# Table blocks as dot products on VectorE, and two of an expert's 42 weight tiles multiplied whole in fp32

## The chip, the cores and the metric

The kernel runs on one core of a Trainium2 chip. The metric is the device time of one execution in microseconds (us): the median of three runs is 1449.65 (1448.9 to 1453.23). The engines are named as in the profile: PE is TensorE's matmuls and PEld its weight loads, DVE is VectorE, ACT is ScalarE, POOL is GpSimd, SP the engine that issues most transfers. A difference of about 0.3% (4.3 us) is what a measurement of this kernel can tell from no change.

## The reference, cut to what matters

Everything is float32. Two layers work on 256 latent tokens of width 1024. In each layer six vectors of 1024 come out of a conditioning vector `c` (the "ada table"); they shift, scale and gate what follows. Layer 0 is differential attention with a short convolution, then a dense SwiGLU (the FFN). Layer 1 is a spatial gating unit (the SGU), then eight SwiGLU experts, of which each token uses two.

```python
def ada_chunks(cond, w, b):                  # w: 1024 x 6144 per layer
    m = jax.nn.silu(cond) @ w + b
    return jnp.split(m, 6, axis=-1)

def moe_swiglu(h, router_w, wg, wu, wd):     # wg, wu: 8 x 1024 x 3584, wd: 8 x 3584 x 1024
    ...
    for e in range(N_EXPERTS):
        out = out + dense_gate[..., e:e + 1] * swiglu(h, wg[e], wu[e], wd[e])
    return out
```

## The kernel before

**Split products.** A weight tile is 128 x 2048 fp32 (1 MB in `raw`, brought by SP's queue). ACT rounds it to fp32r (the high part, `mh`), DVE subtracts to get the low part (`ml`), and PE multiplies in fp32r: high by high, high by low, low by high (`mm3`, L141 to L144), three products of 512 columns for each 128 x 512 piece.

**The experts** (L912 to L1338). Each has 42 tiles: in each of 7 chunks of 512 hidden columns two tiles of the gate matrix, two of the up matrix, and two of the down matrix, which is multiplied two chunks later (LAG = 2). One chunk's six tiles make a step: gate, up, down. An expert with at most 64 tokens is *light*: its tokens' high and low parts stand side by side as 128 columns, so two products do the work of three (`products`, L1083, lines L1089 and L1090). Otherwise it is *heavy* (lines L142 to L144). PE chooses between the two by a branch at each group of two tiles. Here the experts run in the order heavy, light, light, light, heavy, heavy, light, light. After a chunk's gate and up products the 128 x 512 results are turned (L1156 light, L1158 heavy), made into `m_sg` (L1162 on ACT, L1163 on DVE) and split into `moe_aT` (L217, L218). Tokens for the next expert are gathered in chunks 4 and 5 (`m_oh` L1110, `m_pg` L1119, `m_xg`); results are put back early in the next expert (`m_yg`, `m_sc`, `moe_acc`).

**Buffers.** Raw tiles stand in a ring of six (five of `raw`, slot 8). High parts have five buffers (four of `hi`, and slot 7 where n % 5 is 4), low parts five. So the high part of tile n goes into the buffer of tile n - 5. `Weights.split` (L948) is called up to three tiles ahead of the group, `Weights.load` six tiles ahead of the split. Each engine takes its instructions in the order in which they stand; SP issues a load when DVE has freed its raw buffer.

**The table.** Of the 24 blocks of 512 columns, eight are multiplied on DVE during the FFN (GROUPS, the entries with a last 0; `ada_v`, L332): rows of the table lie on the partitions, so a half block of 4 x 512 columns takes four operations that multiply by one value of silu(c) per partition and add to a running sum (L341, L343), and when both halves are done four small matmuls with a column of ones add up over the partitions (L349), and DVE adds the bias (L351).

Of the kernel before, what the change touches and what calls it, by code (L numbers as in the profile page):

```python
# [37 lines left out]
BEFORE_FFN, BEFORE_SGU = 1, 3  # L38

STAGES = ((0, 2), (2, 4), (4, 6), (6, 8))  # L40

# [33 lines left out]
def hybrid_kernel(  # L75
    ctx: ExitStack, tc: tile.TileContext, consts, params, heads, x_t, ctx_t, sgu_ws_t, router_t, ada_b, sgu_b_s,
    ada_w, ada_pairs, w_qk, w_in_even, w_out_even,
    ffn_w_gate, ffn_w_up, ffn_w_down, sgu_w_in, sgu_w_out,
# [170 lines left out]
    waiting, due = [], [0.0]  # L249
    gf1 = gp.tile([P, D], F32, name="gf1")  # L250

# [54 lines left out]
    def ada(blocks, n):  # L306


        layer, n0 = blocks[0]
        nb, b = len(blocks), n - n0  # L310
        if b == 0:
            held[0] = bank(f"ada{layer}_{n}", psd)
        pa = held[0]
        ada_mm(pa, cS[:, :, 3 - b:35 - b], None, layer, n, b == 0, b == nb - 1)
        if b < nb - 1:
            flush()
            return
# [4 lines left out]
        nc.sync.dma_start(gf1, ada_b[1:2, 5 * D:6 * D].partition_broadcast(P))  # L322

        def gate():
            for o in range(2):
                T.matmul(pa, selb[o], rw, start=True, stop=True)
                v = gf1[:, o * 512:o * 512 + 512]
                V.tensor_tensor(v, pa, v, op=ALU.add)

        waiting.append(gate)  # L330

    def ada_v(layer, n, half):  # L332

        r = ada_load(layer, n, half)
        if half == 0:
            held[0] = next_rows()
        ac = held[0]
        for j in range(4):
            k = 4 * half + j
            if k == 0:  # L340
                V.tensor_scalar(ac, r[:, j, :], cT[:, k, 0:1], None, op0=ALU.mult)  # L341
            else:
                V.scalar_tensor_tensor(ac, r[:, j, :], cT[:, k, 0:1], ac, op0=ALU.mult, op1=ALU.add)  # L343
        flush()
        if half:
            def cols_of():
                pa = bank(f"adv{layer}_{n}_c", psd)
                for i in range(4):
                    T.matmul(pa[:, i:i + 1], ac[:, i * P:(i + 1) * P], ones[:, 0:1], start=True, stop=True)  # L349
                c = R_ADA + layer * 48 + n * 4  # L350
                V.tensor_tensor(modT[:, layer, n // 2, (n % 2) * 4:(n % 2) * 4 + 4, 0], pa[:, :4], cols[:, c:c + 4], op=ALU.add)  # L351

            waiting.append(cols_of)

# [274 lines left out]
    for s, (k0, k1) in enumerate(STAGES):  # L629
# [4 lines left out]
        if s == 0:  # L634
            nc.sync.dma_start(trig, consts[:, C_COS:C_W])
            nc.sync.dma_start(early[:, 256:640], heads.partition_broadcast(P))
        modulated(ctxT, rc, m_c, hc, k0, k1, "xc")
        w = split(qk, f"qk{k0}")
# [277 lines left out]
    class Weights:  # L916

        def __init__(self):  # L920
            self.tiles, self.groups, self.raw, self.parts = [], [], {}, {}
            for e in range(NE):
                for ci in range(NCH):
                    for m in range(2):
                        self.add([((moe_w_gate, moe_w_up)[m][e, ci, half], 4) for half in range(2)])
                    if e or ci >= LAG:
                        self.add(self.down(*divmod(e * NCH + ci - LAG, NCH)))
# [4 lines left out]
            self.loads = self.splits = 0  # L932

# [7 lines left out]

        def load(self, upto):
            while self.loads < min(upto, len(self.tiles)):
                n = self.loads
                self.raw[n] = load(*self.tiles[n], f"mw{n}", None if n % 6 < 5 else 8)
                self.loads += 1

        def split(self, upto):  # L948
            while self.splits < min(upto, len(self.tiles)):
                n = self.splits  # L950
                self.load(n + 1)
                r = self.raw.pop(n)
# [5 lines left out]
                self.parts[n] = hi, lo  # L958
                self.splits += 1

# [136 lines left out]
    class Expert:  # L1097


        def __init__(self, e, pos, xg_slot, n):  # L1100
            self.e, self.n, self.pos = e, n, pos
            self.aT, self.part = {}, {}
            self.xg = in_pairs(slot(xg_slot, n + "_xg", F32R)[:, :2 * KT * P], KT)
# [56 lines left out]
        def act(self, ci, pts):  # L1160
            sg = x2k(f"{self.n}_{ci}_sg")
            A.activation(sg, pts[0], AF.Silu)  # L1162
            V.tensor_tensor(sg, pts[1], sg, op=ALU.mult)  # L1163

            def cut():
                self.aT[ci] = in_pairs(at[((self.e * NCH if isinstance(self.e, int) else 0) + ci) % 3], 4)
                split_pairs(self.aT[ci], sg)

            return cut

        def down(self, ci, parts, light):
            aT = self.aT[ci]
# [12 lines left out]
        def gated(self, i):  # L1185
            src = x2k(f"{self.n}_yg{i}")
            V.tensor_tensor(src, self.y[i], gf1[:, i * 512:(i + 1) * 512], op=ALU.mult)
            return src
# [32 lines left out]
    behind["V"] = ex.made.ins  # L1221
    W.load(8)
    lights = [None] * NE
# [6 lines left out]
    def group(light, body):  # L1230
# [3 lines left out]
        for n in range(tiles.stop + 1, tiles.stop + 4):  # L1234
            W.split(n)
            W.load(n + 6)
            if n == tiles.stop + 2:
# [144 lines left out]
def laid_out(inputs):  # L1382
# [8 lines left out]
    pairs = i["ada_w"][0, :, :2 * D].reshape(2, 4, P, 2, 4, 256).transpose(4, 0, 2, 1, 3, 5).reshape(4, 2, P, 2048)  # L1391

    def ffn_up(w):
        whole = tiles(w[0, :, :2560], 4, 512).transpose(1, 0, 2, 3).reshape(10, P, 2048)
# [4 lines left out]
             "sgu_ws_t": i["sgu_w_s"][0].transpose(2, 0, 1), "router_t": i["router_w"][0].reshape(KT, P, NE).transpose(1, 0, 2),  # L1399
             "ada_b": i["ada_b"], "sgu_b_s": i["sgu_b_s"],  # L1400
             "ada_w": tiles(i["ada_w"], 4, 512), "ada_pairs": pairs,
             "w_qk": tiles(w_in[:, :1024], 2, 1024), "w_in_even": tiles(w_in[:, 1024:], 4, 512), "w_out_even": tiles(i["w_out_even"][0], 4, 512),
# [21 lines left out]
```

## Time and profile before

The page is of one execution that took 1453.82 us, with a span of 1452.0 us between its first and last instruction.

| engine | busy us | share of the span |
|---|---|---|
| PE | 1382.3 | 95% |
| PEld | 1149.5 | 79% |
| DVE | 1213.6 | 84% |
| ACT | 986.2 | 68% |
| POOL | 1.9 | 0% |

The shares are means over stages with different limits: the first 209 us are attention and convolution, the FFN runs to about 400 us, the SGU to about 508 us, and the experts fill the rest. TensorE's granted clock is 0.99 of its upper level (2.4 GHz) over the span. Busy time of pipelined matmuls counts each from its start to its modelled end, so the distance between the starts of two matmuls in a row is what one costs PE.

### The profile page before, as it was taken

The page shows a single profiled execution, that of the slowest core. Times are in us where ns is not written, and L with a number is a line of the kernel's source. Part 1 is how long each engine was busy: PE and PEld are TensorE (multiplying, and loading weights), DVE is VectorE, ACT ScalarE, POOL GpSimd, SP SyncE. Part 2 cuts the span into 40 slices and gives each one's busy share as a digit, 9 for nine tenths or more (in the row PEclk, how much of TensorE's full clock was granted, in tenths as well). Part 3 has the DMA queues.
Part 4 walks back from the last instruction along what each step waited for, and adds up shares of the span by engine and source line. Part 5 has one row for each costly group of instructions (what it writes and reads, how often), then busy time and mean ns, then how long its engine had stood idle before and what let it go on. Part 6 is the DMA issues. An engine that isn't in the chain of part 4 may idle for free.

```text
span 1452.0 us, 19805 instructions
## 1 busy us (share of the span) xinstructions
PE 1382.3 (95%) x7746; PEld 1149.5 (79%) x7746; DVE 1213.6 (84%) x1208; ACT 986.2 (68%) x927; POOL 1.9 (0%) x7
## 2 busy tenths in 40 slices
PE   6999999999999999998998998999999999999896
PEld 4667789999979788886777876778888888777674
DVE  5687588776667597789999999999888888999997
ACT  3444354334355587787898988987787678798895
POOL 0000000000000000000000000000000000000000
PEclk9999999999999999999999999999999999999999
DMA  9654388877664588899999999999999889999994
GB/s 374 230 212 179 139 343 320 304 266 267 232 230 176 218 342 343 321 375 353 401 403 398 402 407 406 385 412 354 362 327 351 327 332 359 400 397 401 407 404 184
DMA packets 66783, 473.52 MB, mean 326 GB/s; under 512 B 7376, under 2 KB 7760, under 8 KB 9696
## 3 DMA queue, kind: packets, MB, share of 16 engines
q1 hardware_dynamic: 66464, 471.16, 83.3%
q8 instruction: 93, 1.52, 0.4%
q0 software_dynamic: 192, 0.56, 0.2%
q14 instruction: 34, 0.28, 0.1%
HBM read 470.64 MB, written 1.05 MB: 325 GB/s over the span
## 4 chain that ended last, share of the span: by engine, by line
PE 62%; DVE 18%; issue 8%; ACT 8%; DMA 4%; SPq 0%; DVEq 0%; ACTq 0%
DVE ml L957 12%; PE m L144 5%; PE m L142 5%; PE m L143 5%; ACT mh L956 5%; PE fg_ps L164 4%; PE fd L164 4%; PE fu_ps L164 4%; PE m_y L142 3%; PE m_y L144 3%; PE m_y L143 3%; PE ada L259 2%; PE so_ps L164 2%; PE su_ps L164 2%; PE m L1090 1%
## 5 line engine op out<-in xcount | busy, mean ns | idle before, releaser
L957 DVE TENSOR_TENSOR ml<-mw,mh 128x2048 fp32r<-128x2048 f32 x336 | 757.0, 2285 | 52.1 <-ACT mh L956 48.9
L956 ACT CAST mh<-mw 128x2048 fp32r<-128x2048 f32 x336 | 632.1, 1911 | 9.2 <-PE so_ps L164 4.1
L1089 PE MATMUL m<-mh,m_xg 128*128 128x512 f32 x560 | 224.5, 401 | 0.0
L1090 PE MATMUL m<-ml,m_xg 128*128 128x512 f32 x560 | 222.3, 397 | 2.3 <-DVE ml L957 2.3
L142 PE MATMUL m<-mh,m_xg 128*128 128x512 f32 x336 | 134.7, 401 | 0.4 <-ACT m_xg L217 0.4
L1090 PE MATMUL m_y<-ml,moe_aT 128*128 128x512 f32 x280 | 116.3, 415 | 18.9 <-DVE ml L957 17.6
L144 PE MATMUL m<-mh,m_xg 128*128 128x512 f32 x336 | 133.1, 396 | 0.0
L143 PE MATMUL m<-ml,m_xg 128*128 128x512 f32 x336 | 132.8, 395 | 0.0
L1090 PEld LDWEIGHTS m<-ml,m_xg 128*128 128x128 f32 x560 | 105.3, 188 | 30.0 <-DVE ml L957 7.1
L1089 PEld LDWEIGHTS m<-mh,m_xg 128*128 128x128 f32 x560 | 105.3, 188 | 22.9 <-issue 0.2
L1089 PE MATMUL m_y<-mh,moe_aT 128*128 128x512 f32 x280 | 111.7, 399 | 3.3 <-DVE moe_aT L218 3.3
L1090 PEld LDWEIGHTS m_y<-ml,moe_aT 128*128 128x128 f32 x280 | 53.1, 190 | 49.6 <-DVE ml L957 39.0
L217 ACT CAST moe_aT<-m_sg 128x512 fp32r<-128x512 f32 x56 | 37.6, 671 | 61.9 <-DVE m_sg L1163 61.2
L144 PEld LDWEIGHTS m<-mh,m_xg 128*128 128x128 f32 x336 | 65.5, 195 | 13.1 <-DVE m_xg L218 0.6
L142 PEld LDWEIGHTS m<-mh,m_xg 128*128 128x128 f32 x336 | 65.7, 195 | 12.5 <-ACT m_xg L217 0.9
L143 PEld LDWEIGHTS m<-ml,m_xg 128*128 128x128 f32 x336 | 65.7, 196 | 11.8
L143 PE MATMUL m_y<-ml,moe_aT 128*128 128x512 f32 x168 | 66.3, 395 | 0.0
L144 PE MATMUL m_y<-mh,moe_aT 128*128 128x512 f32 x168 | 66.3, 395 | 0.0
L142 PE MATMUL m_y<-mh,moe_aT 128*128 128x512 f32 x168 | 65.8, 395 | 0.0
L1089 PEld LDWEIGHTS m_y<-mh,moe_aT 128*128 128x128 f32 x280 | 53.2, 190 | 14.3 <-issue 3.7
L164 PE MATMUL fd<-a,fd_hi 128*128 128x256 f32 x352 | 63.0, 281 | 0.0
L1162 ACT ACTIVATE m_sg<-m_t 128x512 f32<-128x512 f32 x56 | 33.5, 599 | 38.8 <-PE m L142 23.5
(406 smaller groups left out, 2670.0 us busy)
## 6 DMA issues: line engine op xcount, KB each, us to landing
mw<-in_moe_w_gate_dram SPq DMA_DIRECT2D x112, 1024.0 KB, 7.5
mw<-in_moe_w_up_dram SPq DMA_DIRECT2D x112, 1024.0 KB, 7.7
mw<-in_moe_w_down_dram SPq DMA_DIRECT2D x110, 1024.0 KB, 7.4
ada<-in_ada_w_dram SPq DMA_DIRECT2D x40, 1024.0 KB, 5.0
fg_w<-in_ffn_w_gate_dram SPq DMA_DIRECT2D x11, 1024.0 KB, 6.0
fu_w<-in_ffn_w_up_dram SPq DMA_DIRECT2D x11, 1024.0 KB, 6.0
fd<-in_ffn_w_down_dram SPq DMA_DIRECT2D x11, 1024.0 KB, 5.1
adap<-in_ada_pairs_dram SPq DMA_DIRECT2D x8, 1024.0 KB, 8.7
```

What stands on the lines that cost most here:

```text
L142: T.matmul(o, lh, rh, start=start, stop=False)
L143: T.matmul(o, lh, rl, start=False, stop=False)
L144: T.matmul(o, ll, rh, start=False, stop=stop)
L164: self.newest = m = T.matmul(o, lhsT, rhs, start=self.first is None, stop=stop, skip_group_check=True)
L217: A.copy(hi, src)
L259: queued(T.matmul(pa[32 * j:32 * j + 32, :r.shape[2]], stat[:, 4 * half + j, :], r[:, j, :], start=(first and half == 0), stop=(last and h ...
L956: queued(A.copy(hi, r), "A")
L957: queued(V.tensor_tensor(lo, r, hi.bitcast(F32), op=ALU.subtract), "V")
L1089: T.matmul(o, x, wh, start=start, stop=False)
L1090: T.matmul(o, x, wl, start=False, stop=stop)
L1162: A.activation(sg, pts[0], AF.Silu)
```

## The change

**In the table,** the eight blocks that DVE multiplies come turned: output columns lie on the partitions and the 1024 inputs along the row. silu(c) is loaded once to all partitions (`cB`, 512 KB from a row of 4 KB) and goes through ACT once. A `tensor_tensor_reduce` of 128 x 1024 multiplies a tile's half by `cB`, adds along the row to a start value, the bias, and writes the finished column of `modT`. The small matmuls and the adding of the bias are gone. `gf1` and `cB` share one buffer, so `gf1`'s load moves from among the first loads to behind the last use of `cB`.

**In the experts,** the second down tile of chunks 2 and 4 (`WHOLE`) isn't split. It is loaded by POOL's queue straight into the high part's buffer of its turn, and multiplied in plain fp32: one product per 128 x 512 piece, against `sg` in a heavy expert, against the pairs in a light one. The ring of raw tiles counts only tiles that are split, still six.

```diff
+WHOLE = (2, 4)
...
-        r = ada_load(layer, n, half)
...
-            if k == 0:
-                V.tensor_scalar(ac, r[:, j, :], cT[:, k, 0:1], None, op0=ALU.mult)
-            else:
-                V.scalar_tensor_tensor(ac, r[:, j, :], cT[:, k, 0:1], ac, op0=ALU.mult, op1=ALU.add)
+        r = load(ada_turned[layer, n, half], 2, f"adt{layer}_{n}_{half}")
+        for j in range(2):
+            b = 4 * n + 2 * half + j
+            V.tensor_tensor_reduce(r[:, j, :], r[:, j, :], cB, 1.0, cols[:, R_ADA + layer * 48 + b:R_ADA + layer * 48 + b + 1],
+                                   op0=ALU.mult, op1=ALU.add, accum_out=modT[:, layer, b // KT, b % KT, 0:1])
         flush()
-        if half:
-            def cols_of():
-                pa = bank(f"adv{layer}_{n}_c", psd)
-                for i in range(4):
-                    T.matmul(pa[:, i:i + 1], ac[:, i * P:(i + 1) * P], ones[:, 0:1], start=True, stop=True)
...
-        def load(self, upto):
-            while self.loads < min(upto, len(self.tiles)):
+        def load(self, most):
+
+            while len(self.raw) < most and self.loads < len(self.tiles):
...
+                if n in self.uncut:
+                    r = splp.tile([P, 2048], F32, tag="hi", name=f"mr{n}", bufs=4) if n % 5 < 4 else slot(7, f"mr{n}")[:, :2048]
+                    src, k = self.tiles[n]
+                    nc.gpsimd.dma_start(r, src)
+                    self.parts[n] = r.rearrange("p (k f) -> p k f", k=k), None
+                    continue
...
+                    if parts[b][1] is None:
+                        k = 2 * b + j
+                        x = aT[:, k, :64, :].rearrange("p s o -> p (s o)").bitcast(F32) if light else sg[:, k * P:(k + 1) * P]
+                        T.matmul(self.y[i], x, parts[b][0][:, j, o], start=False, stop=False)
+                        continue
```

How the order changes. First DVE in the FFN, before: table blocks 11 (`ada_11`, both halves) and 10 (its bias) among the splits of the FFN's weights.

```order
L341 TENSOR_SCALAR ada_rows<-ada_11_0_2254,cT 128x512
L343 SCALAR_TENSOR_TENSOR ada_rows<-ada_11_0_2254,cT,ada_rows 128x512
L218 TENSOR_TENSOR a_2120<-sg_2121,a_2119 128x512
L801 TENSOR_TENSOR sg_2126<-fu_ps_2004,sg_2126 128x512
L343 SCALAR_TENSOR_TENSOR ada_rows<-ada_11_0_2254,cT,ada_rows 128x512 x2
L127 TENSOR_TENSOR fu_w_lo<-fu_w_2268,fu_w_hi 128x2048
L218 TENSOR_TENSOR a_2120<-sg_2126,a_2119 128x512
L127 TENSOR_TENSOR fu_w_lo<-fu_w_2322,fu_w_hi 128x2048
L343 SCALAR_TENSOR_TENSOR ada_rows<-ada_11_1_2376,cT,ada_rows 128x512 x4
L351 TENSOR_TENSOR modT<-adv_10_c,cols 128x4
```

The same place after the change (`adt_11` is the turned block, `ISA` the reducing operation and behind it the reading of its sum):

```order
L345 ISA adt_11_0_2252,modT<-adt_11_0_2252,cB,cols 128x1024
L345 ISA modT 128x1
L220 TENSOR_TENSOR a_2118<-sg_2119,a_2117 128x512
L796 TENSOR_TENSOR sg_2124<-fu_ps_2004,sg_2124 128x512
L345 ISA adt_11_0_2252,modT<-adt_11_0_2252,cB,cols 128x1024
L345 ISA modT 128x1
L129 TENSOR_TENSOR fu_w_lo<-fu_w_2258,fu_w_hi 128x2048
L220 TENSOR_TENSOR a_2118<-sg_2124,a_2117 128x512
L129 TENSOR_TENSOR fu_w_lo<-fu_w_2312,fu_w_hi 128x2048
L345 ISA adt_11_1_2366,modT<-adt_11_1_2366,cB,cols 128x1024
```

Four operations of 512 columns per half block become two of 1024 and two readings, at the same places. Second, PE in the FFN before: block 10's small matmuls stand between the gate and up products.

```order
L164 MATMUL fg_ps_2145<-hf_lo,fg_w_hi 128x256
L164 MATMUL fg_ps_2145<-hf_hi,fg_w_lo 128x256
L349 MATMUL adv_10_c<-cst,ada_rows 128x1 x4
L164 MATMUL fu_ps_2266<-hf_hi,fu_w_hi 128x256
L164 MATMUL fu_ps_2266<-hf_lo,fu_w_hi 128x256
```

The eight rows like the third are gone. Third, PE after the change, at the end of the down group of expert 1, chunk 2: first the light arm's last rows, then the heavy arm's (`mh` and `ml` are the first tile's parts, `mr` is the whole second tile).

```order
L1097 MATMUL m_y_6235<-mh_6506,moe_aT 128x512
L1098 MATMUL m_y_6235<-ml_6507,moe_aT 128x512
L1190 MATMUL m_y_6234<-mr_6570,moe_aT 128x512
L1190 MATMUL m_y_6235<-mr_6570,moe_aT 128x512
L1190 MATMUL m_y_6234<-mr_6570,moe_aT 128x512
L1190 MATMUL m_y_6235<-mr_6570,moe_aT 128x512
L1225 UNCONDITIONAL_BRANCH
...
L146 MATMUL m_y_6235<-mh_6506,moe_aT 128x512
L1190 MATMUL m_y_6234<-mr_6570,m_2_sg 128x512
L1190 MATMUL m_y_6235<-mr_6570,m_2_sg 128x512
L1190 MATMUL m_y_6234<-mr_6570,m_2_sg 128x512
L1190 MATMUL m_y_6235<-mr_6570,m_2_sg 128x512
```

Before, the second tile stood there with eight fp32r matmuls in the light arm and twelve in the heavy one; now with four fp32 matmuls in either.

## Rows read from the trace of the kernel before

**Rows 1.** The page's first part: busy us, share of the span, instructions of each engine.
```profile
PE 1382.3 (95%) x7746; PEld 1149.5 (79%) x7746; DVE 1213.6 (84%) x1208; ACT 986.2 (68%) x927; POOL 1.9 (0%) x7
```
**Rows 2.** Windows: stretch, length, PE, PEld, DVE, ACT, POOL busy, clock, DMA share, GB/s.
```profile
209.00:400.00 191.00, 191.00 (x1625) 191.00 (x1625) 140.00 (x149) 78.79 (x64) 0.00 (x0) 1.00 0.74 275
...
720.00:830.00 110.00, 102.11 (x492) 81.44 (x491) 108.50 (x71) 96.19 (x84) 0.00 (x0) 0.98 1.00 400
...
970.00:1100.00 130.00, 128.90 (x600) 108.57 (x599) 111.28 (x72) 100.10 (x85) 0.00 (x0) 1.00 0.94 354
```
**Rows 3.** Who waited for whom, 720 to 940 us: us in total, times, longest.
```profile
PEld m_y L1090 <- DVE ml L957: 18.4, 22, 1.4
...
DVE ml L957 <- ACT mh L956: 3.3, 9, 0.7
...
ACT mh L956 <- DMA mw<-in_moe_w_up_dram: 0.2, 1, 0.2
```
**Rows 4.** The same for SP's queue, 720 to 940 us.
```profile
SPq L116 <- DVE ml L957: 181.9, 82, 3.1
```
**Rows 5.** DMA, 720 to 940 us: GB/s in 40 equal slices.
```profile
GB/s 363 380 347 408 427 422 416 425 422 420 420 405 368 350 344 419 427 420 423 404 374 359 404 420 422 420 416 423 419 425 416 392 375 407 322 405 419 426 420 372
```
**Rows 6.** Timeline of PE in the FFN: start us, us, what.
```profile
243.23 0.95 PE L349 MATMUL adv_c<-cst,ada_rows 128*128 128x1 f32 x8
244.05 0.36 PE L164 MATMUL fu_ps<-hf_hi,fu_w_hi 128*128 128x256 f32 x1
```
**Rows 7.** DVE groups by form: count, busy us, mean ns, idle before.
```profile
L957 DVE TENSOR_TENSOR ml<-mw,mh 128x2048 fp32r<-128x2048 f32 x336 | 757.0, 2285 | 52.1 <-ACT mh L956 48.9 <-PE so_ps L164 2.8
L343 DVE SCALAR_TENSOR_TENSOR ada_rows<-ada,cT,ada_rows 128x512 f32<-128x512 f32 x56 | 42.0, 749 | 1.2
L218 DVE TENSOR_TENSOR moe_aT<-m_sg,moe_aT 128x512 fp32r<-128x512 f32 x56 | 38.4, 685 | 0.0
...
L341 DVE TENSOR_SCALAR ada_rows<-ada,cT 128x512 f32<-128x512 f32 x8 | 3.8, 478 | 0.0
```
**Rows 8.** Timeline of ACT, second stage of the first projection.
```profile
35.67 0.91 ACT L451 ACTIVATE hc_hi<-xc_m,modT 128x256 fp32r<-128x256 f32 x2 [3.62 <-DVE xc_m L450]
```
**Rows 9.** Timeline of PE in a heavy expert; 20 matmuls stand between these two.
```profile
1010.54 0.40 PE L144 MATMUL m<-mh,m_xg 128*128 128x512 f32 x1
...
1015.43 0.40 PE L144 MATMUL m<-mh,m_xg 128*128 128x512 f32 x1
```
**Rows 10.** PE groups by form: count, busy us, mean ns.
```profile
L778 PE MATMUL sgu_rows<-sgu_s,cst 128*128 128x512 f32 x2 | 1.1, 644 | 0.0
```
**Rows 11.** Timeline of PE, a gather of eight fp32 matmuls.
```profile
821.14 1.95 PE L1119 MATMUL m_pg<-m_oh,h 128*128 128x128 f32 x16
```
**Rows 12.** Timeline of DVE, second light expert: four splits in a row; a chunk's product.
```profile
794.40 8.90 DVE L957 TENSOR_TENSOR ml<-mw,mh 128x2048 fp32r<-128x2048 f32 x4 [0.21 <-ACT mh L956]
803.22 0.68 DVE L1163 TENSOR_TENSOR m_sg<-m_t,m_sg 128x512 f32<-128x512 f32 x1
```
**Rows 13.** Timeline of PE in a light expert's chunk-4 step, second light expert.
```profile
801.18 0.40 PE L1090 MATMUL m<-ml,m_xg 128*128 128x512 f32 x1
...
802.12 0.39 PE L1090 MATMUL m<-ml,m_xg 128*128 128x512 f32 x1
...
810.68 0.40 PE L1089 MATMUL m_y<-mh,moe_aT 128*128 128x512 f32 x1
```
**Rows 14.** DMA, 170 to 179 us: queues (packets, MB, share of 16 engines), POOL's landings.
```profile
q1 hardware_dynamic: 187, 1.36, 37.7%
q0 software_dynamic: 160, 0.52, 32.5%
...
sgu_s<-in_sgu_ws_t_dram POOLq DMA_DIRECT2D x1, 256.0 KB, 2.9
sgu_s<-in_sgu_b_s_dram POOLq DMA_DIRECT2D x1, 256.0 KB, 6.1
```
**Rows 15.** The page's DMA issues: count, KB each, median us from issue to landing.
```profile
ada<-in_ada_w_dram SPq DMA_DIRECT2D x40, 1024.0 KB, 5.0
```

More of the change, by code (lines that the diff above doesn't have):

```diff
@@ L75, in hybrid_kernel @@
 def hybrid_kernel(
-    ctx: ExitStack, tc: tile.TileContext, consts, params, heads, x_t, ctx_t, sgu_ws_t, router_t, ada_b, sgu_b_s,
-    ada_w, ada_pairs, w_qk, w_in_even, w_out_even,
+    ctx: ExitStack, tc: tile.TileContext, consts, params, heads, x_t, ctx_t, sgu_ws_t, router_t, ada_b, c_row, sgu_b_s,
+    ada_w, ada_turned, ada_pairs, w_qk, w_in_even, w_out_even,
     ffn_w_gate, ffn_w_up, ffn_w_down, sgu_w_in, sgu_w_out,
@@ L249, in hybrid_kernel, with row_of_c @@
     waiting, due = [], [0.0]
-    gf1 = gp.tile([P, D], F32, name="gf1")
+    gf1 = []
+    cB = gp.tile([P, D], F32, tag="row", name="cB")
+    def row_of_c():
+        nc.sync.dma_start(cB, c_row.partition_broadcast(P))
+        A.activation(cB, cB, AF.Silu)
     def ada_load(layer, n, half, own=None):
@@ L321, in ada @@
             return
-        nc.sync.dma_start(gf1, ada_b[1:2, 5 * D:6 * D].partition_broadcast(P))
+        gf1.append(gp.tile([P, D], F32, tag="row", name="gf1"))
+        nc.sync.dma_start(gf1[0], ada_b[1:2, 5 * D:6 * D].partition_broadcast(P))
         def gate():
@@ L332, in ada_v @@
     def ada_v(layer, n, half):
-        r = ada_load(layer, n, half)
[L335 to L339, printed above, removed]
-            if k == 0:
-                V.tensor_scalar(ac, r[:, j, :], cT[:, k, 0:1], None, op0=ALU.mult)
-            else:
-                V.scalar_tensor_tensor(ac, r[:, j, :], cT[:, k, 0:1], ac, op0=ALU.mult, op1=ALU.add)
-        flush()
-        if half:
-            def cols_of():
-                pa = bank(f"adv{layer}_{n}_c", psd)
-                for i in range(4):
-                    T.matmul(pa[:, i:i + 1], ac[:, i * P:(i + 1) * P], ones[:, 0:1], start=True, stop=True)
-                c = R_ADA + layer * 48 + n * 4
-                V.tensor_tensor(modT[:, layer, n // 2, (n % 2) * 4:(n % 2) * 4 + 4, 0], pa[:, :4], cols[:, c:c + 4], op=ALU.add)
-            waiting.append(cols_of)
+        r = load(ada_turned[layer, n, half], 2, f"adt{layer}_{n}_{half}")
[3 more added lines that the diff above has]
+                                   op0=ALU.mult, op1=ALU.add, accum_out=modT[:, layer, b // KT, b % KT, 0:1])
+        flush()
     todo = []
@@ L636, in hybrid_kernel @@
             nc.sync.dma_start(early[:, 256:640], heads.partition_broadcast(P))
+            row_of_c()
         modulated(ctxT, rc, m_c, hc, k0, k1, "xc")
@@ L920, in __init__ @@
         def __init__(self):
-            self.tiles, self.groups, self.raw, self.parts = [], [], {}, {}
+            self.tiles, self.groups, self.raw, self.parts, self.uncut = [], [], {}, {}, set()
             for e in range(NE):
@@ L926, in __init__ @@
                     if e or ci >= LAG:
-                        self.add(self.down(*divmod(e * NCH + ci - LAG, NCH)))
+                        at_ = divmod(e * NCH + ci - LAG, NCH)
+                        self.add(self.down(*at_))
+                        if at_[1] in WHOLE:
+                            self.uncut.add(len(self.tiles) - 1)
             for ci in range(NCH - LAG, NCH - 1):
@@ L931, in __init__ @@
                 self.add([([moe_w_down[NE - 1, 2 * NCH - 2 + u].rearrange("p (k f) -> p k f", k=2)[:, :, i * 512:(i + 1) * 512] for u in range(2)], 4)])
-            self.loads = self.splits = 0
+            self.loads = self.splits = self.cut = 0
         @staticmethod
@@ L940, in add @@
             self.tiles += tiles
-        def load(self, upto):
-            while self.loads < min(upto, len(self.tiles)):
+        def load(self, most):
+            while len(self.raw) < most and self.loads < len(self.tiles):
                 n = self.loads
-                self.raw[n] = load(*self.tiles[n], f"mw{n}", None if n % 6 < 5 else 8)
+                if n not in self.uncut:
+                    self.raw[n] = load(*self.tiles[n], f"mw{n}", None if self.cut % 6 < 5 else 8)
+                    self.cut += 1
                 self.loads += 1
@@ L950, in split @@
                 n = self.splits
-                self.load(n + 1)
+                self.splits += 1
+                if n in self.uncut:
[4 more added lines that the diff above has]
+                    continue
+                self.load(1)
                 r = self.raw.pop(n)
@@ L958, in split @@
                 self.parts[n] = hi, lo
-                self.splits += 1
     W = Weights()
@@ L1101, in __init__ @@
             self.e, self.n, self.pos = e, n, pos
-            self.aT, self.part = {}, {}
+            self.aT, self.sg, self.part = {}, {}, {}
             self.xg = in_pairs(slot(xg_slot, n + "_xg", F32R)[:, :2 * KT * P], KT)
@@ L1163, in act @@
             V.tensor_tensor(sg, pts[1], sg, op=ALU.mult)
+            self.sg[ci] = sg
             def cut():
@@ L1171, in down @@
         def down(self, ci, parts, light):
-            aT = self.aT[ci]
+            aT, sg = self.aT[ci], self.sg[ci]
             for b in range(2):
@@ L1221, in hybrid_kernel @@
     behind["V"] = ex.made.ins
-    W.load(8)
+    W.load(6)
     lights = [None] * NE
@@ L1235, in group @@
             W.split(n)
-            W.load(n + 6)
+            W.load(6)
             if n == tiles.stop + 2:
@@ L1399, in laid_out @@
              "sgu_ws_t": i["sgu_w_s"][0].transpose(2, 0, 1), "router_t": i["router_w"][0].reshape(KT, P, NE).transpose(1, 0, 2),
-             "ada_b": i["ada_b"], "sgu_b_s": i["sgu_b_s"],
-             "ada_w": tiles(i["ada_w"], 4, 512), "ada_pairs": pairs,
+             "ada_b": i["ada_b"], "c_row": i["c"], "sgu_b_s": i["sgu_b_s"],
+             "ada_w": tiles(i["ada_w"], 4, 512), "ada_turned": turned, "ada_pairs": pairs,
              "w_qk": tiles(w_in[:, :1024], 2, 1024), "w_in_even": tiles(w_in[:, 1024:], 4, 512), "w_out_even": tiles(i["w_out_even"][0], 4, 512),
```

5 lines of the change are left out of this document (3 added, 2 removed).

## The prediction

> **What bounds the kernel now.** The page's shares come first [rows 1]: PE 95% and DVE 84% say only that both matter. Which of them ends last is read by stage, so next come the windows [rows 2]. In the FFN (209 to 400 us) PE is busy 191.0 of 191.0 us and DVE 140.0: PE sets the time, DVE has 51 us to spare. In a heavy expert (970 to 1100) PE is busy 128.9 of 130 and DVE 111: PE again. In a light one (720 to 830, one full period) DVE is busy 108.5 of 110, PE 102.1, and the transfers run at 400 GB/s with a share of 1.00. Three resources lie within 8% there, so third I read who waits [rows 3]: PE's weight loads wait for DVE's low parts (18.4 us in two experts), DVE waits 3.3 us for ACT, ACT 0.2 us for a transfer. SP's queue itself waits for DVE to free raw buffers, 181.9 of 220 us [rows 4]. So DVE ends last in a light expert. The transfers are close: 42 tiles of 1024 KB are 44.0 MB, at the 420 to 427 GB/s of the best slices [rows 5] 103 to 105 us against 110.
>
> **The table.** Each of eight blocks puts its four small matmuls (eight records) into a stretch where PE never idles. They start at 243.23, the next product at 244.05 [rows 6]; without the four that product would start where they do. So 0.82 us go at each place, 0.82 x 8 = 6.6 us in all, on the path, since PE is the only engine at its limit there.
>
> On DVE 42.0 + 3.8 us of multiply-adds go [rows 7]. In their place stand 32 reducing operations of 128x1024, of which the trace has none. From below: two-input rows cost 685 ns at 512 and 2285 at 2048 columns [rows 7], which is 1.04 ns a column and 0.15 us fixed: 1.22 us at 1024 and 0.15 for the reading of one sum, 32 x 1.37 = 44 us. From above: a second pass over the product, 32 x 2.6 = 83 us. I take the lower end, because the nearest row, the multiply-add with two fp32 inputs (749 ns at 512), pays nothing extra for its second operation. At 44 us DVE's sum in the FFN is unchanged; at 83 it is 177 of the 185 us that are left, still below PE, but with bursts of 5 us between splits, which is a rival below.
> The Trainium skill speaks against my choice (Vector Engine (DVE) Microarchitecture Reference, section "Points that are easy to get wrong"): scalar-tensor-tensor forms with two non-bf16 SBUF inputs run at half rate, as no port is left for the accumulator. By it a reduction would take 2.3 us (an estimate from that page), 32 of them 73 us. The 749 ns row does not show half rate, but it accumulates nothing, so the trace doesn't settle it.
>
> The load of `cB` (512 KB) adds one transfer to SP's first dozen, and one ACT operation between the copy and `hc_hi` in the second stage of the projection. ACT stands idle 3.62 us there [rows 8], and 128x1024 costs it about 1 us. I count 0; without that cover it is 1 to 2 us, and DVE's splits of `qk` stand a place later there as well. From below it is -1.
>
> **The whole tiles, heavy experts.** A tile is four 128x512 pieces. As fp32r each takes three products; 21 starts lie in 4.89 us [rows 9], 0.233 each, so a tile costs PE 12 x 0.233 = 2.79 us. In fp32 the trace records each matmul twice: the one 512-column fp32 matmul has two records of 644 ns that cover 1.1 us [rows 10], so the second starts 0.456 after the first. The gather's 16 records in 1.95 us [rows 11], of 128 columns, make 0.49 at four times the width, or 0.45 without the last one's tail. With 0.456 a tile takes 8 x 0.456 = 3.65 us. PE pays +0.86 a tile (0.8 to 1.1), all on its path: 2 x 3 x 0.86 = +5.2 us (4.7 to 6.8). What DVE and ACT save there is worth nothing.
>
> **The whole tiles, light experts.** DVE loses two splits of 2.20 us each (four take 8.90 [rows 12]): -4.4 us per expert on the engine that ends last. PE pays 3.65 less eight products of 0.235 [rows 13], +1.77 a tile, 3.5 per expert. That is why the gain isn't 4.4. PE's sum goes from 102 to 105.6, DVE's from 108.5 to 104.1. Worse, both sit in the same two steps, those of chunks 4 and 6: there DVE's work falls and PE's rises, so PE ends last in them. The step of chunk 4 holds a turning and half a gather (16 records of 128 columns each, 1.95 us as [rows 11]) and six tiles: 15.2 us of PE work before, 16.9 after, while DVE's falls by 2.2. DVE's relief becomes time only if DVE can run ahead there and use the lead in the first chunks of the next expert, where it does the putting back. The lead is limited: `m_sg` of the next chunk stands two or three splits ahead in DVE's order [rows 12] and needs PE's turning first. So the bounds per light expert are -4.4 (all of the lead is kept) and 0 (none). The transfers' floor of 103 to 105 us would allow -5 to -7 and doesn't cut these. I take -2.5, a little above the middle, as the step of chunk 6 has no gather and keeps its own relief: 5 x -2.5 = -12.5 us (-22 to 0).
>
> **POOL's load** must be there when PE comes to the tile. It can start when PE has done tile n - 5, the first gate tile of the same step: its last product starts at 802.12, the second down tile's first at 810.68 [rows 13], so 8.4 us remain, and behind the waiting load on POOL stands nothing else. PE would wait, and behind it the turning, and DVE's `m_sg`. No 1 MB load by POOL is in the trace. Between 170 and 179 us POOL's queue moved 0.52 MB in 160 packets while SP's moved 1.36 MB in 187 [rows 14]: about as many packets each, smaller ones for POOL, whose rows there were 2 KB. With rows of 8 KB like SP's it should get half of 420 GB/s, 5.0 us; a 1 MB load on SP's queue in quieter stretches lands after 5.0 us [rows 15], 2.5 more than 420 GB/s takes, so 2.5 for issue and completion: 7.5 us, in time with 0.9 left. From above, at the rate of that row (two 256 KB loads in 6.6 us, the second landing 6.1 after its issue) 1 MB takes 13 us. I take 7.5, since the tile's rows are as long as SP's.
>
> **The sum,** against the profiled execution: 1453.8 - 6.6 + 5.2 - 12.5 = 1439.9 us. That execution is 4.2 above the median of the runs, so I put the change, -13.9, on the median: 1449.65 - 13.9 = 1435.8 us. A difference of 0.3%, 4.3 us, is about what a measurement here can tell.
>
> **Rivals.**
> 1. DVE keeps the whole lead: light experts fall by 4.4 each. For it: DVE is busy 98.6% of the period and PE's sum stays near 105. Against: the order of `m_sg`. -6.6 + 5.2 - 22 = -23.4, 1426.2 us.
> 2. The light experts gain nothing: PE in the two steps and the transfers (share 1.00, best slices no higher than 427 GB/s) take it all. -6.6 + 5.2 = -1.4, 1448.2 us, no change that can be told.
> 3. The reducing operations take two passes, and PE waits for the FFN's splits behind them. For it: an operation the trace doesn't have. Against: DVE has 51 us spare. The 6.6 us are gone: 1442.4 us or a little more.
> 4. The whole tiles come late, the slower side. If a load takes 13 us, PE stands 4.6 us at each of ten light tiles: with the +3.5 of fp32 an expert's PE gets 12.7 more, of which its 8 us of idle time take up 8. Light experts +4.7 each, 23 in all: -6.6 + 5.2 + 23 = +22, 1471 us. It begins to decide where a landing takes more than about 10.7 us: there 4.6 us of waiting in two tiles and 3.5 of fp32 fill PE's idle time, and the sum is near 0.
> The Trainium skill has a mechanism for this (SBUF — State Buffer, section "SBUF: two separate sides"): a transfer issued by GpSimd needs descriptors that GpSimd writes into SBUF, and certain DVE operations lock it out of the port until they end, so the transfer seems blocked by DVE. DVE runs two-input splits almost without a gap where POOL's loads fall, but the page names its two-port modes for this, which the splits aren't; no run here shows it. Were each load held up for a split in progress, 2.2 us, it would land 9.7 us after its issue, 1.3 too late and below the 10.7 at which lateness decides; that is part of the chance I give this rival.
>
> **Chances.** Forecast 0.51 (its own range 1430 to 1443, which also holds most of rival 3 at 0.07); rival 1 0.17; rival 2 0.14; rival 4 0.11. Faster by over 0.3%: forecast, rivals 1 and 3, 0.75. Within 0.3%: rival 2 without its slower edge, 0.14. Slower: 0.11. For 8 in 10 the range takes in rival 1 and reaches just past rival 2: 1425 to 1450 us.
>
> **What would show it.** Right: no records between the FFN's gate and up products, and the FFN shorter by 6 us with DVE's busy time there within 5 us of 140; the fp32 products of a whole tile start 0.46 us apart; heavy experts 1.7 us longer each, light periods 106 to 109 us with DVE's waits on PE grown; POOL's loads land 7 to 9 us after issue and PE hardly waits for them. Wrong: light periods still at 110 (rival 2) or at 105.6 (rival 1); reducing operations over 2 us and PE idle in the FFN; waits of PE's down products for POOL's transfers of several us each.

## The result and the profile after

The changed kernel takes 1502.26 us (median of 4, 1500.66 to 1506.37) against 1451.44 on the same chip: 1.0352 times as long, 95% interval 1.0332 to 1.0372. Forecast were 1435.8. Below, a ratio is always against the kernel before on the same chip, and 0.1% of it is 1.45 us.

The page's shares after, to be held against [rows 1]:

```profile
PE 1398.7 (93%) x7658; PEld 1142.5 (76%) x7658; DVE 1174.5 (78%) x1184; ACT 959.2 (64%) x912; POOL 10.4 (1%) x23
```

DVE is busy 39 us less, PE 16 us more, and the span is 50 us longer: the shares of PE, DVE and ACT all fell, so these engines wait more for each other. Where, the windows say (columns as in [rows 2]): the FFN's stretch, one light expert (the period that lay at 737.5 to 847.6 before), that expert's steps of chunks 4, 5 and 6, and a heavy expert.

```profile
209.00:400.00 191.00, 190.88 (x1618) 188.48 (x1618) 140.21 (x157) 82.82 (x73) 0.00 (x0) 1.00 0.76 288
...
739.90:860.50 120.60, 105.31 (x491) 80.54 (x490) 103.79 (x68) 92.69 (x81) 1.06 (x2) 0.99 0.92 365
...
799.90:819.80 19.90, 16.98 (x68) 11.39 (x68) 18.36 (x14) 13.14 (x11) 0.53 (x1) 0.91 1.00 404
819.80:841.20 21.40, 17.13 (x98) 14.18 (x96) 8.56 (x6) 12.72 (x18) 0.00 (x0) 1.00 0.58 223
841.20:860.50 19.30, 15.96 (x67) 10.68 (x67) 19.09 (x12) 17.61 (x14) 0.53 (x1) 1.00 1.00 395
...
979.00:1112.80 133.80, 127.93 (x578) 104.29 (x578) 105.85 (x70) 93.33 (x81) 1.06 (x2) 1.00 0.86 331
```

The light period went from 110 to 120.6 us with PE at 105.3 and DVE at 103.8, almost the sums that were forecast (105.6 and 104.1): neither engine got more work than expected, both stand still. In chunk 5's step DVE works 8.6 of 21.4 us and the transfers fall to a share of 0.58; before, the step took 14.8 us:

```profile
817.30:832.10 14.80, 14.80 (x84) 12.63 (x82) 13.51 (x10) 14.64 (x17) 0.00 (x0) 1.00 1.01 411
```

The experts one by one, from the transposes of its one-hot rows (`m_ohp`) to those of the next expert's (the last to the end of the span), in us:

| kernel | heavy 0 | light 1 | light 2 | light 3 | heavy 4 | heavy 5 | light 6 | light 7 |
|---|---|---|---|---|---|---|---|---|
| before | 118.4 | 112.3 | 110.0 | 110.0 | 127.1 | 130.8 | 109.2 | 127.4 |
| after | 121.0 | 121.4 | 120.6 | 118.6 | 133.8 | 137.8 | 122.3 | 128.6 |

They lose 59 us in all. The first loses 2.6 and the last 1.2; the six between lose 7 to 13 each, heavy ones too. What sets the first and the last apart is the gather of the next expert's tokens: the last has none, and the first kept its order. PE's order in the others, before and after, shown on one of them (`m_pg` is the gather, `m_4_t` the turning of chunk 4; the numbers are places in PE's list, equal rows merged):

```
before: 4047 L1211 UNCONDITIONAL_BRANCH
        4048 L1119 MATMUL m_pg_6871<-m_oh,h 128x128 x8
        4049 L1211 COMPARE_AND_BRANCH
        4050 L1156 MATMUL m_4_t_6792<-fold,m_4_g 128x128 x4
after:  4010 L1225 UNCONDITIONAL_BRANCH
        4011 L1127 MATMUL m_pg_6754<-m_oh,h 128x128
        4012 L1225 COMPARE_AND_BRANCH
        4013 L1164 MATMUL m_4_t_6675<-fold,m_4_g 128x128 x4
        ...  (chunk 5's gate products)
        4059 L1127 MATMUL m_pg_6754<-m_oh,h 128x128 x7
        4060 L1127 MATMUL m_pg_6826<-m_oh,h 128x128 x5
        ...  (chunk 5's up products)
        4104 L1127 MATMUL m_pg_6826<-m_oh,h 128x128 x3
```

The gather's first half, in one piece between two groups before, is torn: one matmul stays, seven go behind the next group, and the second half is torn too. On ACT the four activations that read it (`m_t`) stay where they were, two roundings behind `m_u`. The timelines of PE, ACT and DVE there (start us, us, what, idle before and its releaser):

```profile
812.77 5.27 PE L1190 MATMUL m_y<-mr,moe_aT 128*128 128x512 f32 x8 [2.25 <-DMA mr<-in_moe_w_down_dram]
817.88 0.39 PE L1127 MATMUL m_pg<-m_oh,h 128*128 128x128 f32 x2
818.10 1.06 PE L1164 MATMUL m_t<-fold,m_g 128*128 128x128 f32 x8
...
823.62 1.72 PE L1127 MATMUL m_pg<-m_oh,h 128*128 128x128 f32 x14
```

```profile
814.38 1.90 ACT L965 CAST mh<-mw 128x2048 fp32r<-128x2048 f32 x1 [0.77 <-DMA mw<-in_moe_w_up_dram]
825.38 1.50 ACT L1133 ACTIVATE m_t<-m_pg,modT,a_m 128x128 f32<-128x128 f32 x4 [9.11 <-PE m_pg L1127]
826.77 1.91 ACT L965 CAST mh<-mw 128x2048 fp32r<-128x2048 f32 x1
```

```profile
816.31 2.29 DVE L966 TENSOR_TENSOR ml<-mw,mh 128x2048 fp32r<-128x2048 f32 x1 [0.34 <-ACT mh L965]
828.71 2.29 DVE L966 TENSOR_TENSOR ml<-mw,mh 128x2048 fp32r<-128x2048 f32 x1 [10.11 <-ACT mh L965]
```

The order of reading: PE stands 2.25 us for the whole tile, multiplies it, does one matmul of the gather (two records), then a turning and a group of products, and only at 823.62 the rest of the first half. ACT has waited for that since 816.3, with the next rounding queued behind; DVE waits for the rounding (10.1 us), and SP's queue for DVE, which empties the transfers. SP's wait in chunk 5's step:

```profile
SPq L118 <- DVE ml L966: 20.9, 3, 12.0
```

From the end of the first expert on, ACT's and DVE's waits are these, two lines from before (600 to 1440 us) and two from after (610 to 1490 us):

```profile
ACT m_t L1125 <- PE m_pg L1119: 13.2, 9, 3.2
...
DVE ml L957 <- ACT mh L956: 35.5, 47, 3.8
...
ACT m_t L1133 <- PE m_pg L1127: 75.3, 12, 10.5
...
DVE ml L966 <- ACT mh L965: 116.5, 51, 10.6
```

The whole tiles themselves (count, ns min/median/max, first and last start):

```profile
L1190 PE MATMUL m_y<-mr,moe_aT x80: 590/592/1220, 693.0 to 1480.5; 128*128 128x512 f32 x80
...
  PE m_y L1190: 13.1, 8
...
DMA to landing us min/median/max: 5.6/9.4/10.7
```

Each product is two records, whose starts lie 0.429 us apart. PE waits 13.1 us in all for eight of the sixteen loads; three times the granted clock is then at its lower level (1.2 GHz), where the starts are 0.853 apart (the longest record, 1220 ns, is one of these).

The reducing operations (same columns):

```profile
L345 DVE CUSTOM_DVE_ANT_0 adt<-adt,cB,cols x32: 1274/1280/1289, 214.0 to 367.8; 128x1024 f32<-128x1024 f32 x32
L345 DVE DVE_READ_ACCUMULATOR2_ANT modT<- x32: 80/83/89, 215.2 to 369.0; 128x1 f32 x32
```

The FFN's first products and its last ones, before and after (same columns):

```profile
L164 PE MATMUL fg_ps<-hf_hi,fg_w_hi x176: 277/280/386, 208.2 to 378.6; 128*128 128x256 f32 x176
L164 PE MATMUL fd<-a,fd_lo x176: 277/281/287, 255.8 to 403.3; 128*128 128x256 f32 x176
...
L166 PE MATMUL fg_ps<-hf_hi,fg_w_hi x176: 277/280/384, 209.1 to 373.4; 128*128 128x256 f32 x176
L166 PE MATMUL fd<-a,fd_lo x176: 277/280/282, 255.7 to 396.1; 128*128 128x256 f32 x176
```

### The profile page after: what moved, and what is told of

It reads as the page before. It is cut to its first block, busy times and chain, and to the rows that moved or that the text cites. A ratio compares the mean times of both kernels' runs of the same rounds, so it can differ in the third digit from the quotient of the medians.

```text
span 1501.5 us, 19617 instructions
## 1 busy us (share of the span) xinstructions
PE 1398.7 (93%) x7658; PEld 1142.5 (76%) x7658; DVE 1174.5 (78%) x1184; ACT 959.2 (64%) x912; POOL 10.4 (1%) x23
## 5 line engine op out<-in xcount | busy, mean ns | idle before, releaser
L966 DVE TENSOR_TENSOR ml<-mw,mh 128x2048 fp32r<-128x2048 f32 x320 | 722.3, 2287 | 136.1 <-ACT mh L965 131.1
L965 ACT CAST mh<-mw 128x2048 fp32r<-128x2048 f32 x320 | 602.9, 1911 | 38.0 <-issue 8.2
L1098 PE MATMUL m_y<-ml,moe_aT 128*128 128x512 f32 x240 | 100.0, 417 | 19.9 <-DVE ml L966 19.9
L1097 PE MATMUL m_y<-mh,moe_aT 128*128 128x512 f32 x240 | 97.6, 407 | 3.5 <-ACT mh L965 3.3
L1098 PEld LDWEIGHTS m_y<-ml,moe_aT 128*128 128x128 f32 x240 | 46.4, 193 | 40.3 <-DVE ml L966 30.6
L1133 ACT ACTIVATE m_t<-m_pg,modT,a_m 128x128 f32<-128x128 f32 x64 | 24.9, 465 | 78.0 <-PE m_pg L1127 78.0
L145 PE MATMUL m_y<-ml,moe_aT 128*128 128x512 f32 x144 | 57.1, 396 | 3.6 <-DVE ml L966 3.6
L144 PE MATMUL m_y<-mh,moe_aT 128*128 128x512 f32 x144 | 57.0, 399 | 1.1 <-ACT mh L965 1.1
L1097 PEld LDWEIGHTS m_y<-mh,moe_aT 128*128 128x128 f32 x240 | 46.2, 193 | 15.2 <-ACT mh L965 5.0
L146 PE MATMUL m_y<-mh,moe_aT 128*128 128x512 f32 x144 | 56.8, 395 | 0.0
```

The costliest lines, as they stand in the source:

```text
L144: T.matmul(o, lh, rh, start=start, stop=False)
L145: T.matmul(o, lh, rl, start=False, stop=False)
L146: T.matmul(o, ll, rh, start=False, stop=stop)
L965: queued(A.copy(hi, r), "A")
L966: queued(V.tensor_tensor(lo, r, hi.bitcast(F32), op=ALU.subtract), "V")
L1097: T.matmul(o, x, wh, start=start, stop=False)
```

## The experiments

Two theories. *Torn gather*: the order of PE's queue is what costs. *Late tile*: POOL's loads land late, and PE's waits are passed on. A third, that the light experts gain nothing whatever is done, came up on the way.

**table_only**: `-WHOLE = (2, 4)` `+WHOLE = ()`.

> The dot products of the table stay, no tile is whole. In the changed kernel the FFN and what follows it ended 9.5 us sooner than before at the first product of the experts, so both theories give 1451 - 9 = 1442 us here (1439 to 1445). Were it 1450 or more, the two parts would not simply add up.

Measured: 1442.65 us, ratio 0.9928 (0.9909 to 0.9947). As expected; the table is worth 10 us, and the whole tiles cost some 61.

**whole_in_chunk_4**: `+WHOLE = (4,)`.

> One whole tile an expert (chunk 4's), where PE's order keeps the 16 products of each half of the gather together, as before. Theory 'torn gather' (the whole tile of chunk 2 makes the order tear the gather apart, ACT stands before its four activations with the roundings queued behind them, and everything behind starves): with the gather in one piece an expert loses nothing worth speaking of, 1442 plus at most 2 us an expert, 1436 to 1455. Theory 'late tile' (PE's waits for POOL's loads, 0.9 to 2.4 us each, are passed on and grow): half of the 59 us lost in the experts stay, 1465 to 1475.

Measured: 1453.17, ratio 1.0011 (0.9997 to 1.0025): 12 us for one whole tile an expert with the gather in one piece, below what *late tile* gave and at the upper edge of *torn gather*'s bounds. The light experts took 114.2, 110.5, 110.8, 112.0 and 125.9 us against 110.9, 110.1, 110.0, 109.2 and 126.4 with the table alone: chunks 0 and 1 gained (13.0 for 13.9 and 14.4), chunk 6's step lost 3 to 4.

**gather_whole**: the one-hot rows of the next expert one chunk sooner.

```diff
-            if ci == NCH - 3 and e + 1 < NE:
+            if ci == NCH - 4 and e + 1 < NE:
                 nxt = experts[e + 1] = Expert(e + 1, posm, (e + 1) % 2, f"m{e + 1}")
                 nxt.positions()
+            if ci == NCH - 3 and e + 1 < NE:
```

> Both whole tiles, loaded by POOL as late as in the changed kernel, but the one-hot rows of the next expert are made one chunk sooner, by which both halves of the gather stand on PE in one piece, the first ahead of chunk 4's down group. Theory 'torn gather': the 6.8 to 13.2 us lost in each of six experts go, 1502 - 55 = about 1447 us, 1435 to 1455. Theory 'late tile': the loads land as late as before and PE waits as much; over 1490.

Measured: 1473.78, ratio 1.0145 (1.0120 to 1.0169): 30 us came back, half of the loss. Neither theory alone. The waits for the gather went, PE's for POOL's loads did not (waits, 610 to 1490 us):

```profile
ACT m_t L1133 <- PE m_pg L1127: 7.1, 6, 1.2
```

```profile
PE m_y L1190 <- DMA mr<-in_moe_w_down_dram: 16.7, 9, 3.2
```

**gather_whole_early_load**: that, and

```diff
-                    r = splp.tile([P, 2048], F32, tag="hi", name=f"mr{n}", bufs=4) if n % 5 < 4 else slot(7, f"mr{n}")[:, :2048]
+                    r = slot(8, f"mr{n}")
...
-                    self.raw[n] = load(*self.tiles[n], f"mw{n}", None if self.cut % 6 < 5 else 8)
+                    self.raw[n] = load(*self.tiles[n], f"mw{n}", None)
...
-            W.load(6)
+            W.load(5)
```

> As the last one, and the whole tiles have a buffer of their own (slot 8, the sixth of the raw ring, which then has five), so that POOL can load one as soon as the one before is done, two steps ahead. Theory 'torn gather': PE's waits for POOL's transfers (13 us in all) go, some of the gain that was forecast comes, 1425 to 1445, unless the ring of five starves DVE. Theory 'late tile': this one alone of the four recovers, 1435 to 1450, and the other with two whole tiles stays over 1490.

Measured: 1457.92, ratio 1.0035 (1.0021 to 1.0049): 16 us more came back, and PE waits for no load of POOL any more. Both causes are real; what is left is still above the table alone. The edit does one thing more: it takes the whole tiles out of the high parts' buffers, so ACT's roundings no longer wait for their products (6.9 us in **gather_whole**, none here). The 16 us are the price of both, and no run parts them.

**early_load_gather_torn**: the early loads without the sooner one-hot rows.

> The changed kernel with the whole tiles in slot 8, so that POOL loads them two steps ahead (raw ring of five); the order of the gather stays torn. The runs so far: torn and late 1502, in one piece and late 1474, in one piece and early 1458. If the tear costs by itself, because ACT's four activations stand in the queue ahead of roundings that DVE needs, it stays at 1480 or more (1458 + 28 = 1486 if the two costs simply add). If the tear only passed on the lateness of the tile just ahead of it, early loads alone bring 1458 to 1466.

Measured: 1493.95, ratio 1.0288 (1.0271 to 1.0305): 37 us above the one in one piece. The tear costs by itself, with no late tile ahead of it; ACT's wait for the gather is nearly as long as in the changed kernel:

```profile
ACT m_t L1133 <- PE m_pg L1127: 65.3, 12, 10.3
```

**table_ring_of_five**: the early loads' ring with `WHOLE = ()`.

> The table alone, no whole tile, with a raw ring of five instead of six: a control for the kernels that give slot 8 to the whole tiles. They lose 15 us against the table alone (1442.65). If the ring is what they pay for, this run shows it: 1450 to 1458. If the price is PE's fp32 products and the order around them, 1442 to 1446.

Measured: 1452.41, ratio 1.0014 (1.0000 to 1.0027): 12 us for the sixth raw buffer. So the 16 us of the early loads were a net figure (28 if the ring's price simply adds), and at an equal ring the whole tiles, early and with the gather in one piece, cost 0.2%, 3 us, which is less than one measurement can tell (0.3%).

**whole_one_pass**: a whole tile's products in fp32r, one for each piece.

```diff
-                        x = aT[:, k, :64, :].rearrange("p s o -> p (s o)").bitcast(F32) if light else sg[:, k * P:(k + 1) * P]
+                        x = aT[:, k, :64, :].rearrange("p s o -> p (s o)") if light else aT[:, k, :, 0]
...
-                    r = slot(8, f"mr{n}")
+                    r = slot(8, f"mr{n}", F32R)
...
-                    nc.gpsimd.dma_start(r, src)
+                    nc.gpsimd.dma_start(r, src.bitcast(F32R))
```

> As the kernel with the gather in one piece and early loads (1458), but a whole tile is multiplied in a single fp32r product for each 128x512 piece, of the tile's own bits: the low parts are left out, so PE pays 4 x 0.233 = 0.93 us for a tile instead of 3.43, and less than for a split one (1.86 in a light expert, 2.79 in a heavy one). DVE and ACT are relieved as before. If PE's fp32 products are the price, the light experts fall under the table's 110 us, to 104 to 107, heavy ones by 2 x 1.86 = 3.7, in all 1442 - 5 x 4 - 3 x 3.7 = 1411, 1405 to 1430. If the ring or the order around the whole tiles is the price, PE's relief brings little: 1438 to 1455.

Measured: 1437.13, ratio 0.9898 (0.9882 to 0.9915): 20 us under the fp32 products, but not the 1405 to 1430. The three heavy experts give 15.8 of it (5.1, 5.6, 5.1). A light one still takes 109 to 112 us, with DVE at 104.6:

```profile
725.40:835.70 110.30, 101.28 (x482) 82.25 (x482) 104.59 (x69) 94.06 (x81) 1.06 (x2) 0.96 1.00 401
```

**one_pass_loaded_once** and **whole_loaded_once**: the last kernel, and the one with early loads, with a single load. Both leave out the weights of all whole tiles but one, so only their times are of use.

```diff
-                    r = slot(8, f"mr{n}")
+                    if not self.once:
+                        self.once.append(slot(8, f"mr{n}"))
+                        nc.gpsimd.dma_start(self.once[0], src)
+                    r = self.once[0]
```

> As the one-pass kernel (1437), but the whole tile is loaded once and every expert multiplies that same one, so an expert loads 40 tiles and not 42. In the one-pass kernel a light period is 109.2 to 112 us with DVE busy 104.6 and PE 101.3; only the transfers have a share of 1.00. If the transfers set it, 40 tiles at the same 403 GB/s take 104.1 us and the five light experts fall by 4 to 5 us each: 1437 - 22 = 1415 (1410 to 1422). If the queues' order sets it, 1432 to 1438.

> As the kernel with the gather in one piece and early loads (1458; the whole tiles multiplied in fp32), but the whole tile is loaded once and every expert multiplies that same one. If the transfers keep the relief of DVE from becoming time, light periods of 111.5 to 115.7 us fall towards DVE's 105 and PE's 103: 1458 - 22 = 1436 (1430 to 1442). If PE's fp32 products and the order around them do, 1452 to 1458.

Measured: 1425.27, ratio 0.9808 (0.9792 to 0.9825), and 1453.94, ratio 1.0013 (1.0001 to 1.0024). Where PE pays nothing extra, two loads fewer are worth 13 us, between the two expectations; where it pays fp32, 3 us. A light expert of the one and of the other:

```profile
720.50:827.50 107.00, 97.28 (x482) 78.68 (x482) 104.38 (x69) 93.87 (x81) 0.00 (x0) 1.00 0.99 393
```

```profile
732.40:843.50 111.10, 102.20 (x490) 80.34 (x491) 104.84 (x69) 93.64 (x81) 0.00 (x0) 1.00 0.98 378
```

With the same relief of DVE and the same number of loads PE's 4.9 us more make 4.1 us of period here, and 2.3 to 4.2 in the other light experts but the last, which is 1.9 us shorter. In the fp32 kernel the place is chunk 6's step (18.3 to 18.7 us, 15.5 with the table alone): it holds a whole tile, the turning of the expert's last chunk behind it, and `m_sg`, for which ACT, DVE and PE's next transposes wait in turn.

**table_onehots_sooner**: the sooner one-hot rows with `WHOLE = ()`.

> The table alone, no whole tile, with the one-hot rows made one chunk sooner. The first half of the gather then stands on PE in one piece ahead of chunk 4's down group, and the second half is torn there: five of its eight ahead of chunk 5's up products, three behind them. If a torn gather costs by itself, it shows without any whole tile: 1450 to 1465 against 1442.65. If the tear hurts only where PE is already late by a whole tile's fp32 products, 1441 to 1446.

Measured: 1446.38, ratio 0.9950 (0.9933 to 0.9967), 3 us above the table alone, with intervals that overlap, and just above the second expectation. So the sooner rows, which **gather_whole** needs, don't bring the 30 us by themselves. Chunk 5's steps, where the second half is torn, take 14.1 us against 14.7; so a tear costs nothing where three matmuls go behind a group. Chunk 3's steps took 17.1 for 14.3. The tear of the changed kernel puts seven of a half's eight behind a group, and ACT's place for them did not move.

**table_ten_blocks**: `(1, 8, 10, 0)` in GROUPS, and **table_ten_other_blocks**: `(1, 0, 2, 0)`, to see whether the table carries further.

> The table alone with ten blocks on VectorE instead of eight: the two (layer 1, blocks 8 and 9) that PE multiplies between the FFN and the SGU, at 396.2 to 403.4 us of the table's run, go the same way. PE loses 32 records that take 4.7 us there and eight small ones of 0.9; DVE gets 8 x 1.36 = 11 us more in the FFN, where it has some 50 to spare. If nothing else is late there, 1442.65 - 5.6 = 1437; if those records only filled the wait for the SGU's norm, 1440 to 1443.

> The table alone with ten blocks on VectorE, as in the run that gave 1447, but the two more are blocks 0 and 1 of layer 1, which PE multiplies at 201.6 to 209 us of the table's run, just ahead of the FFN; blocks 8 and 9, which there filled PE's wait for the SGU's norm (5.6 us when they were gone, and the granted clock at half for 13.7 us), stay with PE. If PE is the only engine at its limit ahead of the FFN, its 32 records go from the path, 0.14 to 0.21 us each: 1442.65 - 5 = 1438 (1436 to 1440). If these too fill a wait, for the FFN's norm, 1442 to 1448.

Measured: 1447.28, ratio 0.9972 (0.9957 to 0.9986), and 1453.44, ratio 1.0008 (0.9994 to 1.0023). Both are worse than eight blocks, and both lie above what was expected. What the expectations took for the cause, that PE's records had only filled its wait for a norm, doesn't explain it: DVE, which got the two blocks, itself comes late to the norm that PE waits for. Of the first kernel PE's wait and the window behind it, then of the second:

```profile
PE hs_ss L166 <- DVE a_m L391: 5.6, 1, 5.6
```

```profile
400.00:416.00 16.00, 7.55 (x23) 6.30 (x24) 13.06 (x45) 5.53 (x14) 0.00 (x0) 0.57 0.48 183
```

```profile
PE hf_bc L413 <- DVE hf_dg L412: 8.6, 1, 8.6
```

```profile
206.00:222.00 16.00, 6.62 (x33) 6.18 (x34) 15.91 (x49) 3.85 (x9) 0.00 (x0) 0.57 0.67 261
```

In the second DVE is busy all the time. Its reducing operations stand among the small steps of the norm, and the last of these steps (`hf_dg`) starts at 213.9 us, with the table alone at 206.0. One of the reducing operations and the step, then the step with the table alone:

```profile
211.02 1.27 DVE L345 CUSTOM_DVE_ANT_0 adt<-adt,cB,cols 128x1024 f32<-128x1024 f32 x1
...
213.94 0.47 DVE L412 TENSOR_SCALAR hf_dg<-cst,hf_v 128x128 f32<-128x128 f32 x2
...
205.98 0.48 DVE L412 TENSOR_SCALAR hf_dg<-cst,hf_v 128x128 f32<-128x128 f32 x2
```

In the first the sums of the norm start 5.9 us behind the FFN's last product, with the table alone 2.9 us. While PE idles in these two places, the granted clock falls to its lower level for 13.7 us of the window (mean 0.57), where it was 1.00 with the table alone.

## Why the prediction was wrong

The sum that the runs give, in ratios: table -0.7%; whole tiles as such, early and with the gather in one piece, +0.2%; late loads +1.1% net, or +2.0% at an equal ring if the ring's price simply adds; the torn gather +2.1%. With 1451 us these are -10, +3, +28 and +30, in all +51. The last two were taken as differences along one path of runs; with early loads the tear cost 37 and not 30, so they don't add up exactly.

- *The table: right in the mechanism, a little short in the size.* The FFN from first to last product went from 195.1 to 187.0 us. Eight places of 0.82 us gave 6.5 of it. At each place the second product behind the small matmuls also started 0.20 us after the first and not 0.12, which the prediction left out: 0.7 in all. The rest is products that stood 0.1175 us apart on average instead of 0.1185, and behind the FFN the way to the experts took 99.6 us with the table alone for 103.5, at a granted clock of 1.00 for 0.95. Neither of these two can be put down to the change: in the profiled execution of **table_onehots_sooner**, which has the same work up to the experts as the table alone, the FFN took 189.1 us and the way to the experts 103.5. So of the 10 us about 6 are read from the trace (7.2 less 0.9 for a later start of the FFN, 209.1 for 208.2), and the rest stays unexplained. The sum for a reducing operation and its reading came out (1.22 + 0.15 forecast, 1.28 + 0.08 measured) because two small misses cancel; rival 3 is out. The half rate that the Trainium skill gives for scalar-tensor-tensor forms with two non-bf16 inputs from SBUF (Vector Engine (DVE) Microarchitecture Reference, "Points that are easy to get wrong") does not show: 2.3 us was the estimate by it. The trace calls the operation CUSTOM_DVE_ANT_0, so it may not be one of those forms.
- *Heavy experts: size of the term right, its scope not.* A tile in fp32 takes 8 x 0.429 = 3.43 us, not 3.65, so +0.64 for +0.86. But "What DVE and ACT save there is worth nothing" let me stop there: the heavy experts with the torn gather lost 6.7 and 7.0, the one where it kept its order 2.6.
- *Light experts: the step that failed.* I wrote that the step of chunk 4 "holds a turning and half a gather (16 records of 128 columns each", from the order of before, counted PE's and DVE's work with it, and took 0 as the worst that could come of it. The sums of work held (105.3 and 103.8 us for 105.6 and 104.1). But the five light experts lost 42.6 us in all where -12.5 was forecast, because PE's queue no longer had the order that I assumed: seven of the eight matmuls of that half stood behind the next group, while ACT's queue kept its place for them. ACT's wait for the gather went from 13.2 to 75.3 us, and keeping the gather in one piece brought back 30 us with late loads and 37 with early ones. The third piece of order shown ahead of the prediction ends at the down group's last row, two rows short of the one matmul that stayed. Where only chunk 2's tile is whole the order tears the gather, where only chunk 4's is it doesn't; the likely reason, argued and not shown, is that the group ahead of the gather no longer waits for a split, so that there is no gap into which the whole half would be put.
- *DVE's lead: rival 2 was right about the light experts.* With the other two causes taken away they show no gain; the kernel as a whole is 0.2% slower at an equal ring. The relief became time only where PE pays nothing for it and the whole tiles aren't loaded again (107.0 us at best, against 110). The -2.5 an expert should have been 0.
- *POOL's load: size wrong, mechanism in part rival 4.* Median 9.4 us to landing, not 7.5, below the 10.7 from which I had lateness decide. That point was wrong: I let PE's idle time absorb the waits, as if an engine's idle time lay where the wait does. PE waited 13 to 17 us, and the runs lost 16 (28 at an equal ring). The Trainium skill's port lock (SBUF — State Buffer, "SBUF: two separate sides") gave an estimate of 9.7, close to the median. But a split didn't hold these loads up: in **gather_whole** one was issued at 1172.70 us, while a split ran from 1172.30 to 1174.59, and by 1174.50 it had moved 0.10 MB. That the loads share the transfers' rate with SP, whose 1 MB loads took 7.0 to 7.6 in the median, is the likely reason; no run shows it.

The version to keep is the table alone: 1442.65 us, faster than both. (**whole_one_pass** is faster still, 1437.13, but it leaves out the low parts of the whole tiles and so computes less exactly.) Not settled: the price of lateness with six raw buffers, since an early load needs a buffer of its own, and the 4 us of the table's gain that the trace doesn't give to the change.

## What to carry to other kernels

When a change alters how long a group takes or what it waits for, compare the whole order of each in-order queue, not only the rows that the diff names: here seven small matmuls in each of six experts, moved behind a group, cost 30 us or more, because another engine's queue had kept its place for them. An engine's idle time in a period absorbs a wait only if it lies at the wait; a sum of busy times that stays below the period promises nothing. And before giving work to an engine with time to spare, look at what stands behind that work in its queue: with ten blocks it was the norm that the other engines wait for.

## What the runs showed of the hardware

- A 1 MB load by POOL landed 9.4 us after its issue in the median (5.6 to 10.7) in the changed kernel, and 9.8 (7.0 to 11.5) with early loads and the gather in one piece, beside medians of SP's 1 MB loads of 6.9 to 7.6. A split in progress on DVE did not stop one of them from moving data.
- A 128x512 product in fp32 is two records that start 0.429 us apart, and 0.853 at the lower clock level. In three of the late tiles, for which PE had stood 1.8 to 2.4 us, the clock was at that level; PE idle for 5.6 and 8.6 us ahead of a norm went with 13.7 us of it.
- A multiply with a sum along the row (128x1024, fp32) takes DVE 1280 ns, and 83 ns for the reading of the sum.
- The same FFN took 187.0 us in some kernels and 189.1 in others, at a granted clock of 1.00 in both: 0.1175 or 0.1188 us from one product to the next in the mean.
- The sixth raw buffer of 1 MB is worth 12 us to the kernel with the table alone.
